# Rotary embedding on one core: 2 MiB units in place of 1 MiB, fp32 stores through ScalarE and SyncE

## The chip, the cores and the metric

The kernel runs on one core of a Trainium2 chip. The metric is the device time of one execution in microseconds (us); 1 us is 1000 ns. An execution is given as the median of several.

## The reference

A rotary position embedding on x of shape (8, 8, 1024, 64), fp32: 64 pairs of batch and head, 1024 positions, 64 values at each. 16.8 MB come in and 16.8 MB go out.

```python
half = x.shape[-1] // 2                       # 32
angles = np.outer(positions * scale, freqs)   # (1024, 32); scale is 0.5
cos, sin = np.cos(angles), np.sin(angles)
x_first, x_second = x[..., :half], x[..., half:]
out_first  = x_first * cos - x_second * sin
out_second = x_first * sin + x_second * cos
out = np.concatenate([out_first, out_second], axis=-1)
```

Positions reach the kernel as 64-bit integers.

## The kernel before

**Units.** A unit is four heads of one batch, 1 MiB of fp32, one contiguous piece of memory. Over 128 partitions each partition has one row of 8 KB: 32 positions of 64 values (`HEADS = 4`, `HP = 32`, `K = 32`, `N = 2048`). There are 16 units (`NU`). Partition p holds positions 32 (p mod 32) and on, so one table of sines and cosines, [128, 32, 32], serves every unit.

**Loads.** Unit 0 comes as fp32 on SP's (SyncE's) queue (L63). The other 15 come in seven DMAs of 1, 1, 2, 2, 3, 3 and 3 units on GpSimd's (POOL's) queue (L78), which cast to fp16 on the way. They are all issued at the start, so all loads stand ahead of every store in that queue. ACT's (ScalarE's) queue brings the positions, the same 8 KB four times, once for each group of 32 partitions (L68), and the row of frequencies (L73).

**Tables.** TensorE spreads the frequencies, times scale / 2 pi, over the partitions (L87, `cfreq`). VectorE (DVE) turns the positions into fp32 (`posf`, L90), multiplies (`y`, L95), and takes off the nearest whole number of turns by adding and subtracting a large constant, once for the sine and once, a quarter turn on, for the cosine (L115, L107, L109). ScalarE takes the sine of both into fp16 tables (L117, L119).

**The loop over units (L124).** Four VectorE instructions a unit: two products of the whole unit with the cosine and with the sine (`pc` L128, `ps` L129, 2048 elements a partition), a difference and a sum of their halves into `OUT`, fp16 (L132, L135, 1024 elements each). `xout` holds ten such buffers. GpSimd's queue stores `OUT` and casts to fp32 on the way (L138). ScalarE has nothing to do in the loop. The tile framework orders the instructions of an engine and places the waits; a buffer is written again only when its last reader has finished, a store when it has landed.

Of the kernel before, what the change touches and what calls it, by code (L numbers as in the profile page):

```python
# [1 line left out]

# [1 line left out]

# [4 lines left out]

FP32 = mybir.dt.float32
FP16 = mybir.dt.float16
I32 = mybir.dt.int32
AF = mybir.ActivationFunctionType
ALU = mybir.AluOpType

_MAGIC = 12582912.0
_TWO_PI_DN = float(np.float32(np.uint32(0x40C90FDA).view(np.float32)))


GROUPS = (1, 1, 2, 2, 3, 3, 3)
BUF_O = 10
BUF_P = 3


@with_exitstack
def kernel(
    ctx: ExitStack,
    tc: tile.TileContext,
    x: bass.AP,  # L30
    freqs: bass.AP,
    positions: bass.AP,
    scale: bass.AP,
    out: bass.AP,
):
    nc = tc.nc

    B, Hh, S, D = x.shape
    NBH = B * Hh
    half = D // 2  # L40
    P = nc.NUM_PARTITIONS
    HEADS = 4
    HP = P // HEADS
    K = S // HP
    N = K * D
    NU = NBH // HEADS
    assert S % HP == 0 and D == 2 * half and NBH % HEADS == 0 and sum(GROUPS) == NU - 1

    fscale = float(scale)

    xv = x.rearrange("b h s d -> (b h s d)").rearrange("(u p n) -> p u n", p=P, n=N)
    ov = out.rearrange("b h s d -> (b h s d)").rearrange("(u p n) -> p u n", p=P, n=N)

    consts = ctx.enter_context(tc.tile_pool(name="consts", bufs=1))
    tmp = ctx.enter_context(tc.tile_pool(name="tmp", bufs=1))
    setup_psum = ctx.enter_context(tc.tile_pool(name="setup_psum", bufs=1, space=bass.MemoryType.PSUM))
    xin = ctx.enter_context(tc.tile_pool(name="xin", bufs=1))
    xout = ctx.enter_context(tc.tile_pool(name="xout", bufs=BUF_O))
    prods = ctx.enter_context(tc.tile_pool(name="prods", bufs=BUF_P))


    X0 = xin.tile([P, N], FP32, name="X0")
    nc.sync.dma_start(out=X0, in_=xv[:, 0, :])  # L63
    xtiles = {0: X0}

    pos_i64 = consts.tile([P, K], positions.dtype)
    for h in range(HEADS):
        nc.scalar.dma_start(  # L68
            out=pos_i64[h * HP : (h + 1) * HP, :],
            in_=positions.rearrange("(q k) -> q k", k=K),  # L70
        )
    freq_row = consts.tile([1, half], FP32)
    nc.scalar.dma_start(out=freq_row, in_=freqs[None, :])  # L73

    u0 = 1
    for g, n in enumerate(GROUPS):
        X = xin.tile([P, n, N], FP16, name=f"X{g + 1}")
        nc.gpsimd.dma_start(out=X, in_=xv[:, u0 : u0 + n, :])  # L78
        for i in range(n):
            xtiles[u0 + i] = X[:, i, :]  # L80
        u0 += n


    coef = consts.tile([1, P], FP32)
    nc.vector.memset(coef, fscale / (2.0 * np.pi))  # L85
    cfreq = setup_psum.tile([P, half], FP32)
    nc.tensor.matmul(out=cfreq, lhsT=coef, rhs=freq_row, start=True, stop=True)  # L87

    posf = consts.tile([P, K], FP32)
    nc.vector.tensor_copy(  # L90
        out=posf,
        in_=pos_i64.bitcast(I32).rearrange("p (k t) -> p k t", t=2)[:, :, 0],
    )
    y = tmp.tile([P, K, half], FP32)
    nc.vector.tensor_tensor(  # L95
        out=y,
        in0=posf.unsqueeze(2).broadcast_to((P, K, half)),
        in1=cfreq.unsqueeze(1).broadcast_to((P, K, half)),
        op=ALU.mult,
    )  # L100

    cosT = consts.tile([P, K, half], FP16)
    sinT = consts.tile([P, K, half], FP16)

    def reduced(src, tag):
        m = tmp.tile([P, K, half], FP32, name="m" + tag)
        nc.vector.tensor_scalar(out=m, in0=src, scalar1=_MAGIC, scalar2=None, op0=ALU.add)  # L107
        rneg = tmp.tile([P, K, half], FP32, name="rneg" + tag)
        nc.vector.scalar_tensor_tensor(  # L109
            out=rneg, in0=m, scalar=_MAGIC, in1=src, op0=ALU.subtract, op1=ALU.subtract  # L110
        )
        return rneg

    yc = tmp.tile([P, K, half], FP32)
    nc.vector.tensor_scalar(out=yc, in0=y, scalar1=0.25, scalar2=None, op0=ALU.add)  # L115
    rc = reduced(yc, "c")
    nc.scalar.activation(out=cosT, in_=rc, func=AF.Sin, bias=0.0, scale=-_TWO_PI_DN)  # L117
    rs = reduced(y, "s")
    nc.scalar.activation(out=sinT, in_=rs, func=AF.Sin, bias=0.0, scale=-_TWO_PI_DN)  # L119
    cos_b = cosT.unsqueeze(2).broadcast_to((P, K, 2, half))  # L120
    sin_b = sinT.unsqueeze(2).broadcast_to((P, K, 2, half))


    for u in range(NU):  # L124
        X = xtiles.pop(u).rearrange("p (k h j) -> p k h j", h=2, j=half)
        pc = prods.tile([P, K, 2, half], FP16, tag="pc")
        ps = prods.tile([P, K, 2, half], FP16, tag="ps")
        nc.vector.tensor_tensor(out=pc, in0=X, in1=cos_b, op=ALU.mult)  # L128
        nc.vector.tensor_tensor(out=ps, in0=X, in1=sin_b, op=ALU.mult)  # L129

        OUT = xout.tile([P, K, 2, half], FP16, tag="O")
        nc.vector.tensor_tensor(  # L132
            out=OUT[:, :, 0, :], in0=pc[:, :, 0, :], in1=ps[:, :, 1, :], op=ALU.subtract
        )
        nc.vector.tensor_tensor(  # L135
            out=OUT[:, :, 1, :], in0=ps[:, :, 0, :], in1=pc[:, :, 1, :], op=ALU.add
        )
        nc.gpsimd.dma_start(out=ov[:, u, :], in_=OUT.rearrange("p k h j -> p (k h j)"))  # L138


# [1 line left out]
_INS = ['x', 'freqs', 'positions', 'scale']  # L142
_OUTS = [((8, 8, 1024, 64), 'float32')]

_NUMBERS = {'scale': 0.5}


# [26 lines left out]
```

## Time and profile before

| what | value |
|---|---|
| median of 11 runs | 85.95 us (85.86 to 86.17) |
| the profiled execution's own time | 85.96 us |
| its span in the profile | 84.2 us |
| VectorE busy | 63.6 us, 76% of the span, 72 instructions |
| ScalarE busy | 3.4 us, 4% |
| GpSimd busy (DMA issue among it) | 13.7 us, 16% |
| HBM read and written | 16.81 MB and 16.78 MB, 399 GB/s over the span |
| GpSimd's DMA queue (q0), share of 16 DMA engines | 99.1% |

The span runs from the first to the last instruction of the profiled execution; its own time has some time outside the span as well. In the profile "DMA" is the busy share of the 16 DMA engines and "GB/s" what they moved, counted at the destination. SPq, ACTq and POOLq are the sequencers that issue DMAs.

### The profile page before, as it was taken

The numbers are of one execution on the slowest core, as the hardware profiler recorded it, in microseconds if no ns is written. First come the engines' busy times: TensorE is split into PE (matmuls) and PEld (weight loads), VectorE is DVE, ScalarE is ACT, GpSimd is POOL, SyncE is SP. The second block draws the span as 40 slices with busy tenths as digits, with TensorE's granted clock in tenths as the row PEclk, the third lists the DMA queues.
The fourth block names the chain that finished last, engine by engine and source line by source line (L and its number), as shares of the span: only waits on it lengthen the run. The fifth ranks groups of instructions, "written<-read, shape, count | busy, mean of one in ns | idle before, by whom it ended". The sixth has DMA issues, their size and how long they took to land.

```text
span 84.2 us, 183 instructions
## 1 busy us (share of the span) xinstructions
PE 0.6 (1%) x2; PEld 0.5 (1%) x2; DVE 63.6 (76%) x72; ACT 3.4 (4%) x3; POOL 13.7 (16%) x27
## 2 busy tenths in 40 slices
PE   0000200000000000000000000000000000000000
PEld 0000100000000000000000000000000000000000
DVE  0000799999999999999999999999999999300000
ACT  0410006300000000000000000000000000000000
POOL 5980000000211202102022020220202202200000
DMA  2899999999999999999999999999999999999970
GB/s 31 311 292 214 208 218 214 212 216 216 214 218 204 218 218 212 214 214 218 177 418 420 436 424 428 424 432 436 420 420 436 420 428 424 436 432 428 420 300 0
DMA packets 4675, 25.73 MB, mean 306 GB/s; under 512 B 578, under 2 KB 578, under 8 KB 2498
## 3 DMA queue, kind: packets, MB, share of 16 engines
q0 software_dynamic: 4336, 24.64, 99.1%
q1 hardware_dynamic: 144, 1.05, 3.6%
q10 hardware_dynamic: 194, 0.03, 0.3%
q14 instruction: 1, 0.01, 0.0%
HBM read 16.81 MB, written 16.78 MB: 399 GB/s over the span
## 4 chain that ended last, share of the span: by engine, by line
DMA 45%; issue 31%; POOL 10%; POOLq 1%
DMA X<-in_x_dram 45%; POOL out_dram L138 5%; POOL X L78 5%; POOLq L169 1%; POOLq L138 0%; POOLq L155 0%
## 5 line engine op out<-in xcount | busy, mean ns | idle before, releaser
L129 DVE TENSOR_TENSOR ps<-X,sinT 128x2048 f16<-128x2048 f16 (+1 forms) x16 | 20.6, 1289 | 0.0
L128 DVE TENSOR_TENSOR pc<-X,cosT 128x2048 f16<-128x2048 f16 (+1 forms) x16 | 20.5, 1287 | 0.0
L138 POOL DMA_DIRECT2D out_dram<-OUT x16 | 8.6, 538 | 58.5 <-DVE OUT L135 58.5
L132 DVE TENSOR_TENSOR OUT<-pc,ps 128x1024 f16<-128x1024 f16 x16 | 11.0, 688 | 0.0
L135 DVE TENSOR_TENSOR OUT<-ps,pc 128x1024 f16<-128x1024 f16 x16 | 11.0, 687 | 0.0
L90 DVE CAST posf<-pos_i 128x32 f32<-128x32 int32 x1 | 0.2, 182 | 7.1 <-DMA pos_i<-in_positions_dram 7.1
L78 POOL DMA_DIRECT2D X<-in_x_dram x7 | 4.9, 714 | 0.8 <-POOLq L155 0.8
L95 DVE TENSOR_TENSOR y<-posf,cfreq 128x1024 f32<-128x1024 f32 x1 | 1.2, 1221 | 0.7 <-PE cfreq L87 0.7
L119 ACT ACTIVATE sinT<-rnegs 128x1024 f16<-128x1024 f32 x1 | 1.1, 1056 | 8.8 <-DVE rnegs L109 8.8
L119 ACT ACT_TABLE_LOAD x1 | 1.3, 1283 | 3.2 <-issue 3.2
L109 DVE SCALAR_TENSOR_TENSOR rnegs<-ms,y 128x1024 f32<-128x1024 f32 x1 | 1.2, 1219 | 0.0
L109 DVE SCALAR_TENSOR_TENSOR rnegc<-mc,yc 128x1024 f32<-128x1024 f32 x1 | 1.2, 1217 | 0.0
L117 ACT ACTIVATE cosT<-rnegc 128x1024 f16<-128x1024 f32 x1 | 1.1, 1057 | 0.1
L85 DVE MEMSET coef<- 1x128 f32 x1 | 0.2, 165 | 0.8 <-PEq L155 0.8
L115 DVE TENSOR_SCALAR yc<-y 128x1024 f32<-128x1024 f32 x1 | 0.7, 693 | 0.0
L107 DVE TENSOR_SCALAR mc<-yc 128x1024 f32<-128x1024 f32 x1 | 0.7, 685 | 0.0
L107 DVE TENSOR_SCALAR ms<-y 128x1024 f32<-128x1024 f32 x1 | 0.7, 684 | 0.0
L87 PE MATMUL cfreq<-freq_row,coef 1*128 1x32 f32 x2 | 0.6, 392 | 8.3 <-DVE posf L90 8.3
L87 PEld LDWEIGHTS cfreq<-freq_row,coef 1*128 1x128 f32 x2 | 0.5, 306 | 8.3 <-DVE posf L90 8.3
L155 POOL MEMSET const-float32-0.0<- 128x1 f32 x1 | 0.1, 98 | 0.2 <-issue 0.2
L155 POOL MEMSET const-bfloat16-1.0<- 128x1 bf16 x1 | 0.1, 101 | 0.0
L155 POOL MEMSET const-float32-1.0<- 128x1 f32 x1 | 0.1, 98 | 0.0
(1 smaller groups left out, 0.1 us busy)
## 6 DMA issues: line engine op xcount, KB each, us to landing
out_dram<-OUT POOLq DMA_DIRECT2D x16, 1024.0 KB, 16.6
X<-in_x_dram POOLq DMA_DIRECT2D x3, 1536.0 KB, 30.6
X<-in_x_dram POOLq DMA_DIRECT2D x2, 1024.0 KB, 15.3
X<-in_x_dram SPq DMA_DIRECT2D x1, 1024.0 KB, 5.0
X<-in_x_dram POOLq DMA_DIRECT2D x2, 512.0 KB, 7.9
pos_i<-in_positions_dram ACTq DMA_DIRECT2D x4, 8.0 KB, 5.0
freq_row<-in_freqs_dram ACTq DMA_DIRECT2D x1, 0.1 KB
```

What stands on the lines that cost most here:

```text
L78: nc.gpsimd.dma_start(out=X, in_=xv[:, u0 : u0 + n, :])
L87: nc.tensor.matmul(out=cfreq, lhsT=coef, rhs=freq_row, start=True, stop=True)
L95: nc.vector.tensor_tensor(out=y, in0=posf.unsqueeze(2).broadcast_to((P, K, half)), in1=cfreq.unsqueeze(1).broadcast_to((P, K, half)), op=A ...
L107: nc.vector.tensor_scalar(out=m, in0=src, scalar1=_MAGIC, scalar2=None, op0=ALU.add)
L109: nc.vector.scalar_tensor_tensor(out=rneg, in0=m, scalar=_MAGIC, in1=src, op0=ALU.subtract, op1=ALU.subtract)
L117: nc.scalar.activation(out=cosT, in_=rc, func=AF.Sin, bias=0.0, scale=-_TWO_PI_DN)
L119: nc.scalar.activation(out=sinT, in_=rs, func=AF.Sin, bias=0.0, scale=-_TWO_PI_DN)
L128: nc.vector.tensor_tensor(out=pc, in0=X, in1=cos_b, op=ALU.mult)
L129: nc.vector.tensor_tensor(out=ps, in0=X, in1=sin_b, op=ALU.mult)
L132: nc.vector.tensor_tensor(out=OUT[:, :, 0, :], in0=pc[:, :, 0, :], in1=ps[:, :, 1, :], op=ALU.subtract)
L135: nc.vector.tensor_tensor(out=OUT[:, :, 1, :], in0=ps[:, :, 0, :], in1=pc[:, :, 1, :], op=ALU.add)
L138: nc.gpsimd.dma_start(out=ov[:, u, :], in_=OUT.rearrange("p k h j -> p (k h j)"))
```

## The change

The kernel is written anew around the same arithmetic:

- A unit is eight heads, 2 MiB; a row is 16 KB, 64 positions a partition. There are eight units, and the table is [128, 64, 32].
- Unit 0 still comes as fp32, half of it on SP's queue, half on ACT's queue behind positions and frequencies. The positions come once, to 16 partitions; TensorE spreads them over the 128 with a mask (`sel`) that GpSimd makes between its first and its second load. ScalarE casts unit 0 to fp16.
- The other seven units are cast loads on GpSimd's queue, one DMA each.
- The cosine comes from the same remainder as the sine: absolute value (a bit operation), then a sine with a bias of a quarter turn.
- Units are worked in the order 1, 2, 0, 3, 4, 5, 6, 7. The four VectorE instructions a unit remain, on twice the elements; all but the sine product write over X.
- ScalarE copies the result into an fp32 buffer `OUT`, of which there are four. Stores move fp32: the first four from GpSimd's queue, the last four from SP's.
- `pin` (`tc.keep_in_program_order`) holds the marked instructions of an engine in the order of the program.

```diff
--- before.py
+++ after.py
@@ -17,10 +17,8 @@
 _MAGIC = 12582912.0
 _TWO_PI_DN = float(np.float32(np.uint32(0x40C90FDA).view(np.float32)))
 
-
-GROUPS = (1, 1, 2, 2, 3, 3, 3)
-BUF_O = 10
-BUF_P = 3
+BUF_O = 4
+BUF_P = 2
 
 
 @with_exitstack
@@ -39,103 +37,113 @@
     NBH = B * Hh
     half = D // 2
     P = nc.NUM_PARTITIONS
-    HEADS = 4
+    HEADS = 8
     HP = P // HEADS
     K = S // HP
     N = K * D
     NU = NBH // HEADS
-    assert S % HP == 0 and D == 2 * half and NBH % HEADS == 0 and sum(GROUPS) == NU - 1
+    assert S % HP == 0 and D == 2 * half and NBH % HEADS == 0
 
     fscale = float(scale)
 
-    xv = x.rearrange("b h s d -> (b h s d)").rearrange("(u p n) -> p u n", p=P, n=N)
-    ov = out.rearrange("b h s d -> (b h s d)").rearrange("(u p n) -> p u n", p=P, n=N)
+    xv = x.rearrange("b h s d -> (b h s d)").rearrange("(u p n) -> u p n", p=P, n=N)
+    ov = out.rearrange("b h s d -> (b h s d)").rearrange("(u p n) -> u p n", p=P, n=N)
 
     consts = ctx.enter_context(tc.tile_pool(name="consts", bufs=1))
     tmp = ctx.enter_context(tc.tile_pool(name="tmp", bufs=1))
-    setup_psum = ctx.enter_context(tc.tile_pool(name="setup_psum", bufs=1, space=bass.MemoryType.PSUM))
+    psum = ctx.enter_context(tc.tile_pool(name="psum", bufs=1, space=bass.MemoryType.PSUM))
     xin = ctx.enter_context(tc.tile_pool(name="xin", bufs=1))
     xout = ctx.enter_context(tc.tile_pool(name="xout", bufs=BUF_O))
     prods = ctx.enter_context(tc.tile_pool(name="prods", bufs=BUF_P))
 
 
-    X0 = xin.tile([P, N], FP32, name="X0")
-    nc.sync.dma_start(out=X0, in_=xv[:, 0, :])
-    xtiles = {0: X0}
 
-    pos_i64 = consts.tile([P, K], positions.dtype)
-    for h in range(HEADS):
-        nc.scalar.dma_start(
-            out=pos_i64[h * HP : (h + 1) * HP, :],
-            in_=positions.rearrange("(q k) -> q k", k=K),
-        )
+    X0f = xin.tile([P, N], FP32, name="X0f")
+    pin = tc.keep_in_program_order
+    nc.sync.dma_start(out=X0f[:, : N // 2], in_=xv[0][:, : N // 2])
+
+    pos_i64 = consts.tile([HP, K], positions.dtype)
+    pin(nc.scalar.dma_start(out=pos_i64, in_=positions.rearrange("(q k) -> q k", k=K)))
     freq_row = consts.tile([1, half], FP32)
-    nc.scalar.dma_start(out=freq_row, in_=freqs[None, :])
+    pin(nc.scalar.dma_start(out=freq_row, in_=freqs[None, :]))
+    pin(nc.scalar.dma_start(out=X0f[:, N // 2 :], in_=xv[0][:, N // 2 :]))
 
-    u0 = 1
-    for g, n in enumerate(GROUPS):
-        X = xin.tile([P, n, N], FP16, name=f"X{g + 1}")
-        nc.gpsimd.dma_start(out=X, in_=xv[:, u0 : u0 + n, :])
-        for i in range(n):
-            xtiles[u0 + i] = X[:, i, :]
-        u0 += n
+    X = [xin.tile([P, K, 2, half], FP16, name=f"X{u}") for u in range(NU)]
+
+    def load(u):
+        nc.gpsimd.dma_start(out=X[u].rearrange("p k h j -> p (k h j)"), in_=xv[u])
+
+
+    sel = consts.tile([HP, HEADS, HP], FP32)
+    load(1)
+    nc.gpsimd.memset(sel, 0.0)
+    nc.gpsimd.affine_select(
+        out=sel, in_=sel, compare_op=ALU.not_equal, fill=1.0, base=0,
+        pattern=[[0, HEADS], [-1, HP]], channel_multiplier=1,
+    )
+    for u in range(2, NU):
+        load(u)
 
 
     coef = consts.tile([1, P], FP32)
-    nc.vector.memset(coef, fscale / (2.0 * np.pi))
-    cfreq = setup_psum.tile([P, half], FP32)
+    pin(nc.vector.memset(coef, fscale / (2.0 * np.pi)))
+    quarter = consts.tile([P, 1], FP32)
+    pin(nc.vector.memset(quarter, np.pi / 2.0))
+    cfreq = psum.tile([P, half], FP32)
     nc.tensor.matmul(out=cfreq, lhsT=coef, rhs=freq_row, start=True, stop=True)
 
+    pos_row = consts.tile([HP, K], FP32)
+    pin(nc.vector.tensor_copy(
+        out=pos_row,
+        in_=pos_i64.bitcast(I32).rearrange("p (k t) -> p k t", t=2)[:, :, 0],
+    ))
+    pos_ps = psum.tile([P, K], FP32)
+    nc.tensor.matmul(
+        out=pos_ps, lhsT=sel.rearrange("q a b -> q (a b)"), rhs=pos_row, start=True, stop=True
+    )
     posf = consts.tile([P, K], FP32)
-    nc.vector.tensor_copy(
-        out=posf,
-        in_=pos_i64.bitcast(I32).rearrange("p (k t) -> p k t", t=2)[:, :, 0],
-    )
+    pin(nc.vector.tensor_copy(out=posf, in_=pos_ps))
+
     y = tmp.tile([P, K, half], FP32)
-    nc.vector.tensor_tensor(
+    pin(nc.vector.tensor_tensor(
         out=y,
         in0=posf.unsqueeze(2).broadcast_to((P, K, half)),
         in1=cfreq.unsqueeze(1).broadcast_to((P, K, half)),
         op=ALU.mult,
-    )
+    ))
+    m = tmp.tile([P, K, half], FP32)
+    pin(nc.vector.tensor_scalar(out=m, in0=y, scalar1=_MAGIC, scalar2=None, op0=ALU.add))
+    r = tmp.tile([P, K, half], FP32)
+    pin(nc.vector.scalar_tensor_tensor(
+        out=r, in0=m, scalar=_MAGIC, in1=y, op0=ALU.subtract, op1=ALU.subtract
+    ))
+    sinT = consts.tile([P, K, half], FP16)
+    pin(nc.scalar.activation(out=sinT, in_=r, func=AF.Sin, bias=0.0, scale=-_TWO_PI_DN))
+    ra = tmp.tile([P, K, half], FP32)
+    pin(nc.vector.tensor_scalar(
+        out=ra.bitcast(I32), in0=r.bitcast(I32), scalar1=0x7FFFFFFF, scalar2=None, op0=ALU.bitwise_and
+    ))
+    cosT = consts.tile([P, K, half], FP16)
+    pin(nc.scalar.activation(out=cosT, in_=ra, func=AF.Sin, bias=quarter, scale=-_TWO_PI_DN))
+    pin(nc.scalar.copy(out=X[0].rearrange("p k h j -> p (k h j)"), in_=X0f))
 
-    cosT = consts.tile([P, K, half], FP16)
-    sinT = consts.tile([P, K, half], FP16)
-
-    def reduced(src, tag):
-        m = tmp.tile([P, K, half], FP32, name="m" + tag)
-        nc.vector.tensor_scalar(out=m, in0=src, scalar1=_MAGIC, scalar2=None, op0=ALU.add)
-        rneg = tmp.tile([P, K, half], FP32, name="rneg" + tag)
-        nc.vector.scalar_tensor_tensor(
-            out=rneg, in0=m, scalar=_MAGIC, in1=src, op0=ALU.subtract, op1=ALU.subtract
-        )
-        return rneg
-
-    yc = tmp.tile([P, K, half], FP32)
-    nc.vector.tensor_scalar(out=yc, in0=y, scalar1=0.25, scalar2=None, op0=ALU.add)
-    rc = reduced(yc, "c")
-    nc.scalar.activation(out=cosT, in_=rc, func=AF.Sin, bias=0.0, scale=-_TWO_PI_DN)
-    rs = reduced(y, "s")
-    nc.scalar.activation(out=sinT, in_=rs, func=AF.Sin, bias=0.0, scale=-_TWO_PI_DN)
     cos_b = cosT.unsqueeze(2).broadcast_to((P, K, 2, half))
     sin_b = sinT.unsqueeze(2).broadcast_to((P, K, 2, half))
 
 
-    for u in range(NU):
-        X = xtiles.pop(u).rearrange("p (k h j) -> p k h j", h=2, j=half)
-        pc = prods.tile([P, K, 2, half], FP16, tag="pc")
+    for i, u in enumerate((1, 2, 0, *range(3, NU))):
         ps = prods.tile([P, K, 2, half], FP16, tag="ps")
-        nc.vector.tensor_tensor(out=pc, in0=X, in1=cos_b, op=ALU.mult)
-        nc.vector.tensor_tensor(out=ps, in0=X, in1=sin_b, op=ALU.mult)
-
-        OUT = xout.tile([P, K, 2, half], FP16, tag="O")
-        nc.vector.tensor_tensor(
-            out=OUT[:, :, 0, :], in0=pc[:, :, 0, :], in1=ps[:, :, 1, :], op=ALU.subtract
-        )
-        nc.vector.tensor_tensor(
-            out=OUT[:, :, 1, :], in0=ps[:, :, 0, :], in1=pc[:, :, 1, :], op=ALU.add
-        )
-        nc.gpsimd.dma_start(out=ov[:, u, :], in_=OUT.rearrange("p k h j -> p (k h j)"))
+        pin(nc.vector.tensor_tensor(out=ps, in0=X[u], in1=sin_b, op=ALU.mult))
+        pin(nc.vector.tensor_tensor(out=X[u], in0=X[u], in1=cos_b, op=ALU.mult))
+        pin(nc.vector.tensor_tensor(
+            out=X[u][:, :, 0, :], in0=X[u][:, :, 0, :], in1=ps[:, :, 1, :], op=ALU.subtract
+        ))
+        pin(nc.vector.tensor_tensor(
+            out=X[u][:, :, 1, :], in0=ps[:, :, 0, :], in1=X[u][:, :, 1, :], op=ALU.add
+        ))
+        OUT = xout.tile([P, N], FP32, tag="O")
+        pin(nc.scalar.copy(out=OUT, in_=X[u].rearrange("p k h j -> p (k h j)")))
+        (nc.gpsimd if i < NU // 2 else nc.sync).dma_start(out=ov[u], in_=OUT)
 
 
 # ---- launch: one core; inputs and outputs as the reference has them ----
```

## The prediction

> **What bounds the kernel now.** First the page: the two DMA rows of the 40 slices (2.1 us each), the queue table, the chain by engine.
>
> ```profile
> span 84.2 us, 183 instructions
> ...
> DVE  0000799999999999999999999999999999300000
> ...
> DMA  2899999999999999999999999999999999999970
> GB/s 31 311 292 214 208 218 214 212 216 216 214 218 204 218 218 212 214 214 218 177 418 420 436 424 428 424 432 436 420 420 436 420 428 424 436 432 428 420 300 0
> ...
> q0 software_dynamic: 4336, 24.64, 99.1%
> ...
> DMA 45%; issue 31%; POOL 10%; POOLq 1%
> ```
>
> The DMA engines are full from slice 2 to slice 37. VectorE (DVE) looks as busy, but stops ten microseconds before the end: it is second. GB/s counts destination bytes: a load that casts to fp16 shows 214 and reads 428, a store shows 428. So both halves run at one rate, 428 GB/s of fp32. The "issue" share of the chain is GpSimd waiting between stores and hides nothing: the transfers behind it had a backlog. The stretches say where DMA time is lost:
>
> ```profile
> core 0: us, PE busy (x) PEld busy (x) DVE busy (x) ACT busy (x) POOL busy (x), PEclk, DMA share, GB/s
> ...
> 1.00:1.50 0.50, 0.00 (x0) 0.00 (x0) 0.00 (x0) 0.00 (x0) 0.26 (x1) 1.00 0.00 0
> ...
> 0.00:5.00 5.00, 0.00 (x0) 0.00 (x0) 0.17 (x1) 1.28 (x1) 3.96 (x10) 1.00 0.61 211
> ...
> 44.00:80.00 36.00, 0.00 (x0) 0.00 (x0) 28.31 (x34) 0.00 (x0) 4.79 (x9) 1.00 1.12 428
> 81.00:81.50 0.50, 0.00 (x0) 0.00 (x0) 0.00 (x0) 0.00 (x0) 0.00 (x0) 1.00 0.80 295
> 81.50:82.00 0.50, 0.00 (x0) 0.00 (x0) 0.00 (x0) 0.00 (x0) 0.00 (x0) 1.00 0.21 66
> 82.00:84.20 2.20, 0.00 (x0) 0.00 (x0) 0.00 (x0) 0.00 (x0) 0.00 (x0) 1.00 0.00 0
> ```
>
> Data flows from about 1.6 to 82.0 us, 80.4 us. Input and output are 33.55 MB; at 428 GB/s that is 78.4 us. The 2.0 us over are a slow start (1.05 MB by 5.0 us instead of 1.46 MB, 0.9 us), an uneven end (0.18 MB in the last microsecond instead of 0.43, 0.6 us), and 0.5 us for the turn from loads to stores and for tiny packets. SP's wait and the landings of the stores say what ends the run:
>
> ```profile
> SPq L169 <- DMA out_dram<-OUT: 81.3, 1, 81.3
> ```
>
> ```profile
> DMA to landing us min/median/max: 9.8/16.6/24.0
> ```
>
> The last store is issued at 72.64 and lands 9.8 us later, at 82.4; the first is issued at 21.5 and lands 24.0 us later, at 45.5, since it stands behind all loads in GpSimd's queue. The span ends 1.7 us after the last landing, and 1.78 us lie outside it (85.96 for a span of 84.18). That run stands at the median (85.95), so I add to 85.96.
>
> **What the Trainium skill says.** "DMA: Bandwidth & Descriptors", section Where 436 GB/s comes from: the ceiling is 435 GB/s over 16 ports; the 428 above agree. The same page, section Why small descriptors are slow (HBM only): each packet has some 3 cycles over its 32-byte beats. An 8 KB row is 256 beats, 301 ns at 850 MHz; one engine's share of 428 GB/s gives 306 ns, so 5 ns a row at most are overhead. The same page, section Queues, rings and completion order: each engine goes round robin between the queues with work, a packet at a time. No row of the trace before shows two large backlogs sharing, so this is taken from the page. "VectorE: DVE Perf Modes", section Side-by-side: where the cycles go for N=2048 bf16, gives 1224 ns for a two-source operation on 16-bit data and 2293 at one element a cycle; here fp16 takes 1222 and fp32 2291.
>
> **The change part by part.** *VectorE.* One unit of now:
>
> ```profile
> 57.03 1.22 DVE L128 TENSOR_TENSOR pc<-X,cosT 128x2048 f16<-128x2048 f16 x1
> 58.16 0.69 DVE L132 TENSOR_TENSOR OUT<-pc,ps 128x1024 f16<-128x1024 f16 x1
> 58.76 0.69 DVE L135 TENSOR_TENSOR OUT<-ps,pc 128x1024 f16<-128x1024 f16 x1
> 59.37 1.22 DVE L129 TENSOR_TENSOR ps<-X,sinT 128x2048 f16<-128x2048 f16 x1
> ```
>
> Starts lie 1.135 us apart for 2048 elements and 0.60 for 1024, also behind a product just written, so working in place should add no wait. 4096 elements take 1.135 + 1.067 = 2.20 (two a cycle at the skill's 0.96 GHz). A new unit takes 2 x 2.20 + 2 x 1.135 = 6.68 us, against 6.95 for two old ones. Half as many instructions save 0.27 us a unit; unit 0 no longer in fp32 saves 2 x 1.07 more. None of it is on the path.
>
> *Set-up.* One positions DMA instead of four.
>
> ```profile
> DMA to landing us min/median/max: 3.4/5.0/5.9
> ```
>
> That row is for the four: each waits for its turn on ACT's queue. I give the only one the shortest, 3.4: it is issued at 0.74 and lands at 4.1 (5.7 with the median). Frequencies follow 0.45 us later, at 4.6, and half of unit 0 behind them. Two matmuls at 0.60 (the present one's time) and a small copy put the angles y at 6.2; y and r have 2048 fp32 elements, 2.29 each (2.20 to the next start), m 1.22 (1.13), so sine starts at 11.9. An ACTIVATE of 1024 elements takes 1.056 now; at the 0.833 ns an element of "ScalarE: Activation LUTs", section What ACT_TABLE_LOAD costs, 2048 take 1.91. The first product starts at 13.9, now 14.4. Units 0 and 1 are 4.2 MB: 1.05 by 5.0 us, the rest at 428, so both have come by 12.8. The mask on GpSimd is not in this trace: between 0.1 us (its memsets) and 2 us, hidden, as the second matmul needs it at 5.3 only. VectorE's units end at 13.9 + 6.68(i+1): 20.6 the first, 47.3 the fifth, 67.3 the last.
>
> *ScalarE.* A copy to fp32 of 4096 elements: 1.056 + 3072 x 0.833 ns = 3.62 us, under VectorE's 6.68, hidden except behind a full set of buffers. The copy of unit 0 ends near 19.5, its product starts at 27.3.
>
> *Stores.* Call them s0 to s7; s0 to s3 stay behind the loads in GpSimd's queue, s4 to s7 go by SP. 2 MiB at 428 GB/s take 4.90. ScalarE has four output buffers, so the copy for s4 waits until s0 has landed, that for s7 until s3 has. Turnaround: landing 0.5, copy 3.62, then SP's issue and start, 0.85 (0.74 to 1.6 for unit 0 now), with waking 5.1 in all. Stores begin near 42.4. s0 ends at 47.3, s1 at 52.2, where s4 begins to share (52.4). Sharing halves s2 and s3: s2 ends at 61.8, s3 at 71.6. By then SP's queue has moved 9.6 us' worth of its 9.8 for s4 and s5, and s6 (copied from 62.4, issued at 66) is behind: 5.1 us of work. s7 can start at 71.6 + 5.1 = 76.7, just when this is used up. So VectorE's 67.3 doesn't matter; the cover of s7's copy is s6, and it has no slack. Bounds on the gap: 0 to 2 us; I take 0.1. What is queued behind the waiting copies on ScalarE is only later copies.
>
> *Rows.* 16 KB instead of 8 KB: an engine's 256 packets become 128, each saving 3.5 ns by the skill's 3 cycles (0.45 us), 5 ns if all excess is by the row (0.64), nothing if rows are cut up or the excess is not by the row. I take 0.3. That a store no longer casts: the byte count on the HBM side is equal and unit 0's uncast load ran at 402 GB/s beside small packets, so 0 (bounds: -0.5 to +1.7, the latter 410 GB/s in 39.2 us of stores). Fewer tiny packets at the start: 0.1 gained. The end is hardware-issued now: 0, from -0.3 to +0.4.
>
> Sum: 85.96 - 0.3 - 0.1 + 0.1 = 85.66, said as **85.65**.
>
> **The rivals.** *A buffer ring that stalls the end (slower).* s7's copy waits for the slowest engine's part of s3. If s3's landing, copy and SP's start take 1.6 us more than the 5.1 us that s6 covers, the DMA idles so long: 87.2. It decides at any excess over 5.1. For it: no slack in my sum; against: were GpSimd's queue served first, s3 would land near 62 and nothing would wait. *Uncast stores that run slower*: twice the SBUF bytes a store; at 410 GB/s 87.6. Against: the skill's ceiling is the same for either. *Rows that don't matter* (the change does not do what it says: rows are cut again, or the 5 ns are not by the row): 85.9. *A better DMA stream*: 0.64 from rows, 0.4 at turn and end: 84.8. *VectorE as the bound*: its end at 67.3 would have to slip beyond 72; lost two-a-cycle speed in place would do it (2 x 2.1 + 2 x 1.07 more a unit), but the shapes are those of now.
>
> **How the numbers follow.** 0.2% (0.17 us) is about what a measurement of this kernel can tell from no change. Likeliest case 0.47 (own range 85.2 to 86.0: faster 0.40, same 0.07); rows that don't matter 0.14 (same 0.09, faster 0.02, slower 0.03); stalled end 0.22 and slow stores 0.10, both slower; better stream 0.07, faster. Together faster 0.49, same 0.16, slower 0.35. The range of all: 84.7 to 87.7.
>
> **What would show it.** Right: DMA tenths of 9 without a dip between 42 and 80, VectorE's last product before 70, ScalarE's copy for s7 waiting on a store's landing near 72, rates of 428 to 432. A dip near 76 shows the stall; rates near 410 slow stores. I am wrong if the first product starts later than 18 or its operations take over 2.4 us.

## The result, and the profile after

The changed kernel takes 84.70 us (median of 8, 84.54 to 84.82) against 85.95 (median of 31): ratio 0.9851, 95% interval 0.9842 to 0.9859. The forecast was 85.65. The direction was right, but the gain is 1.25 us, four times the 0.3 forecast.

The page after, the lines that answer to those shown of before, and the second queue that now stores:

```profile
span 83.3 us, 154 instructions
...
DVE  0008996999999999999999999999999996000000
...
DMA  3899999999999999999999999999999999999990
GB/s 59 283 330 275 295 283 224 220 212 220 216 212 216 212 216 212 224 216 208 142 370 433 417 448 417 448 425 433 433 417 448 417 448 425 433 433 417 448 393 8
...
q0 software_dynamic: 1584, 15.73, 66.6%
q1 hardware_dynamic: 720, 9.44, 27.4%
...
DVE 72%; ACT 7%; DMA 5%; DVEq 1%; PE 1%; issue 1%; ACTq 1%
```

DMA is full as before. Stores show 417 to 448 a slice, mean 432 (it was 428). VectorE heads the chain, since its last product releases ScalarE's last copy and that the last store; what hides behind this, the backlog on SP's queue, the chain doesn't show. The experiments measure it.

This profiled execution took 85.09 us, 0.4 above the median: one DMA engine ended 0.4 us after the rest. A second profile of the same kernel (`after_again`, 84.58 us) doesn't have this and is used from here on. Its stretches, in the columns of the table of stretches before:

```profile
0.00:5.00 5.00, 0.00 (x0) 0.00 (x0) 0.40 (x3) 1.28 (x1) 3.87 (x12) 1.00 0.67 215
...
44.00:70.00 26.00, 0.00 (x0) 0.00 (x0) 25.72 (x16) 13.05 (x4) 0.53 (x1) 1.00 1.01 432
44.00:80.00 36.00, 0.00 (x0) 0.00 (x0) 26.00 (x16) 16.65 (x5) 0.53 (x1) 1.00 1.01 431
```

The first five microseconds are hardly better than before (215 for 211), the stores are a little faster (431 for 428 in the same stretch). Its stores on the output tensor:

```profile
L146 SPq DMA_DIRECT2D out_dram<-OUT x4: 332/332/337, 53.2 to 74.0; - x4
...
DMA to landing us min/median/max: 7.9/16.3/22.1
```

The last store is issued at 74.0 and lands 7.9 us later, at 81.9; before it was 82.4. The span of this execution is 82.8 us. So in this profile 0.5 us of the gain lie ahead of the last landing and 0.85 behind it: from landing to the end of the span it was 1.75 us and is 0.9. The 0.85 is the firm part: in the first profile after, the last landing is at 82.4 as before the change, and 0.84 of its 0.87 us of gain lie behind it. The view of the kernel's last line (the end of the program; start times of the first and last of each kind stand behind the durations) shows what happens there. Before:

```profile
L169 SPq EVENT_SEMAPHORE  x10: 17/28/28, 82.4 to 84.1; - x10
L169 POOLq EVENT_SEMAPHORE  x4: 17/17/17, 83.5 to 84.1; - x4
L169 POOLq DRAIN  x3: 45/93/10803, 72.6 to 83.9; - x3
```

After (second profile):

```profile
L177 SPq EVENT_SEMAPHORE  x11: 17/28/28, 74.4 to 82.7; - x11
L177 POOLq EVENT_SEMAPHORE  x4: 17/17/17, 82.1 to 82.7; - x4
L177 POOLq DRAIN  x3: 45/93/21937, 46.5 to 82.5; - x3
```

GpSimd's first DRAIN starts behind its last store and holds it until its own queue is done. Before it starts at 72.61 and takes 10.80 us: it ends at 83.42, 0.98 us after the last landing, and only then does GpSimd join the others at the end (83.5). After, it ends at 46.5 + 21.9 = 68.4, long before the last landing, and GpSimd joins at 82.1.

SP comes second. An EVENT_SEMAPHORE of SP is here a wait, for a DMA's landing or for the other engines. Before, eight waits for landings lie behind the last landing, 0.06 us apart: the first starts at 82.45, the last ends at 82.92, half a microsecond ahead of GpSimd's DRAIN. After, only one does; the others began at 74.4 and were through before. So the 0.85 needed both. Had the DRAIN alone gone, the seven more waits would have left an end of about 1.33 us (an estimate: 0.89 and seven times 0.0625); kernels below with three and five such waits end at 1.01 and 1.14, as this counting gives.

These lines of before stood in the trace when the prediction was made.

Below, "end" is the time from the last landing (the trace's DMA records) to the end of the span. Between the span and the device time lie 1.78 us in both kernels (84.18 to 85.96, 82.80 to 84.58).

### The profile page after: what moved, and what is told of

Read it like the earlier page. It is cut to its first block, busy times and chain, and to the rows that moved or that the text cites. A ratio compares the mean times of both kernels' runs of the same rounds, so it can differ in the third digit from the quotient of the medians.

```text
span 83.3 us, 154 instructions
## 1 busy us (share of the span) xinstructions
PE 1.1 (1%) x4; PEld 0.9 (1%) x4; DVE 62.6 (75%) x40; ACT 37.4 (45%) x12; POOL 6.7 (8%) x17
## 4 chain that ended last, share of the span: by engine, by line
DVE 72%; ACT 7%; DMA 5%; DVEq 1%; PE 1%; issue 1%; ACTq 1%
DVE X L137 22%; DVE ps L136 21%; DVE X L138 12%; DVE X L141 10%; DMA freq_row<-in_freqs_dram 5%; ACT OUT L145 4%; DVE r L117 3%; DVE y L108 3%; ACT sinT L121 2%; DVE m L115 1%; DVEq L177 1%; PE cfreq L93 1%; PE pos_ps L101 1%; ACTq L66 0%; DVE posf L105 0%
## 5 line engine op out<-in xcount | busy, mean ns | idle before, releaser
L145 ACT CAST OUT<-X 128x4096 f32<-128x4096 f16 x8 | 28.8, 3606 | 25.0 <-DVE X L141 25.0
L136 DVE TENSOR_TENSOR ps<-X,sinT 128x4096 f16<-128x4096 f16 x8 | 18.3, 2285 | 0.7 <-ACT sinT L121 0.7
L137 DVE TENSOR_TENSOR X<-X,cosT 128x4096 f16<-128x4096 f16 x8 | 18.3, 2292 | 0.3
L138 DVE TENSOR_TENSOR X<-X,ps 128x2048 f16<-128x2048 f16 x8 | 9.8, 1225 | 0.3
L141 DVE TENSOR_TENSOR X<-ps,X 128x2048 f16<-128x2048 f16 x8 | 9.7, 1218 | 0.0
L146 POOL DMA_DIRECT2D out_dram<-OUT x4 | 2.1, 534 | 39.1 <-ACT OUT L145 39.1
L128 ACT CAST X<-X0f 128x4096 f16<-128x4096 f32 x1 | 3.6, 3590 | 0.0
L117 DVE SCALAR_TENSOR_TENSOR r<-m,y 128x2048 f32<-128x2048 f32 x1 | 2.3, 2293 | 0.0
L108 DVE TENSOR_TENSOR y<-posf,cfreq 128x2048 f32<-128x2048 f32 x1 | 2.3, 2289 | 0.0
L127 ACT ACTIVATE cosT<-ra,quarter 128x2048 f16<-128x2048 f32 x1 | 2.0, 1987 | 0.0
```

The source lines that it names most:

```text
L108: pin(nc.vector.tensor_tensor(out=y, in0=posf.unsqueeze(2).broadcast_to((P, K, half)), in1=cfreq.unsqueeze(1).broadcast_to((P, K, half)), ...
L117: pin(nc.vector.scalar_tensor_tensor(out=r, in0=m, scalar=_MAGIC, in1=y, op0=ALU.subtract, op1=ALU.subtract))
L128: pin(nc.scalar.copy(out=X[0].rearrange("p k h j -> p (k h j)"), in_=X0f))
L136: pin(nc.vector.tensor_tensor(out=ps, in0=X[u], in1=sin_b, op=ALU.mult))
L137: pin(nc.vector.tensor_tensor(out=X[u], in0=X[u], in1=cos_b, op=ALU.mult))
L138: pin(nc.vector.tensor_tensor(out=X[u][:, :, 0, :], in0=X[u][:, :, 0, :], in1=ps[:, :, 1, :], op=ALU.subtract))
```

## The experiments

All are made from the changed kernel, but for `b_half_sp`. The times are medians beside the kernel before on the same chip (85.89 to 86.01).

**`all_pool`: all stores from GpSimd.**

```diff
-        (nc.gpsimd if i < NU // 2 else nc.sync).dma_start(out=ov[u], in_=OUT)
+        nc.gpsimd.dma_start(out=ov[u], in_=OUT)
```

> All eight fp32 stores go by GpSimd's queue instead of four. Theory (the end): in the profile before, GpSimd's last wait ends about 1.0 us after the last store has landed, in the profile after 0.2 us, since its own queue had finished long before; so most of the gain lies behind the last landing. Then this kernel loses about 0.85 us: 85.5 us, with about 1.7 us from the last landing to the end of the span. Rival (the stream): hardware-issued stores or uncast stores move data faster; then the time from the last landing to the end is not what changes, stores here run at 428 instead of 432 GB/s in the last 20 us, and the loss is at most 0.2 us: 84.9.

Measured: 85.09 us. The last landing is at 81.9, as in the second profile after. The end is 1.39 us:

```profile
L177 POOLq DRAIN  x3: 45/88/8389, 74.2 to 83.0; - x3
```

The DRAIN ends at 82.56, 0.65 us after the landing. So the engine that issues does nothing for the stream, and about 0.45 us for the end (0.5 by the profiles): half of what was expected, for 0.65 is less than the 0.98 of before. `pool_split` below asks why.

**`cast_pool`: no copies on ScalarE, casting stores from GpSimd.**

```diff
-        OUT = xout.tile([P, N], FP32, tag="O")
-        pin(nc.scalar.copy(out=OUT, in_=X[u].rearrange("p k h j -> p (k h j)")))
-        (nc.gpsimd if i < NU // 2 else nc.sync).dma_start(out=ov[u], in_=OUT)
+        nc.gpsimd.dma_start(out=ov[u], in_=X[u].rearrange("p k h j -> p (k h j)"))
```

> As after the change, but stores are fp16 from X, cast to fp32 by GpSimd's DMA as in the kernel before; ScalarE copies nothing in the loop and all eight stores go by GpSimd. If stores that don't cast neither gain nor lose, this equals the kernel with all fp32 stores by GpSimd: 85.1. If casting slows the stream (the 428 GB/s of before against 434), 85.4 to 85.6. If the end depends on the cast, the time from the last landing to the end differs from 1.39 us.

Measured: 85.12 us, last landing 81.9, end 1.39: equal to `all_pool` in all three. A store that casts is neither slower nor faster. So ScalarE's copies earn nothing by themselves; in the changed kernel they serve the stores on SP's queue.

**`rows8`: rows of 8 KB again.**

```diff
-        nc.gpsimd.dma_start(out=X[u].rearrange("p k h j -> p (k h j)"), in_=xv[u])
+        xf = X[u].rearrange("p k h j -> p (k h j)")
+        for c in (slice(0, N // 2), slice(N // 2, N)):
+            nc.gpsimd.dma_start(out=xf[:, c], in_=xv[u][:, c])
...
-        (nc.gpsimd if i < NU // 2 else nc.sync).dma_start(out=ov[u], in_=OUT)
+        for c in (slice(0, N // 2), slice(N // 2, N)):
+            (nc.gpsimd if i < NU // 2 else nc.sync).dma_start(out=ov[u][:, c], in_=OUT[:, c])
```

> Every load on GpSimd's queue and every store is cut into two DMAs of half the columns, so that rows are 8 KB again; all else is as after the change. Theory: rows give the part of the gain that the end does not, 3.5 to 5 ns for each of 128 more packets an engine, 0.45 to 0.6 us: 85.2. Rival: the row length does nothing and the stream is faster for the engine that issues or for lack of a cast: 84.7.

Measured: 85.38 us, 0.75 above `after_again` (84.63, on another chip). The stretch of stores:

```profile
44.00:70.00 26.00, 0.00 (x0) 0.00 (x0) 25.72 (x16) 13.05 (x4) 1.05 (x2) 1.00 1.01 428
```

428 GB/s, as before the change, and the last landing is at 82.3. Only a part of the 0.75 us is the rows. 0.25 us is the end, 1.14 here: after the last landing SP still has four more waits, 0.06 us each, for DMAs that have long landed. Another 0.27 us lies outside the span, 2.05 us in this kernel and 1.77 to 1.78 in every other profile; why is open. That leaves 0.23 us for the stream by the medians. By the landings it is 0.4 against the second profile after, and 0.3 against the mean (82.0) of the six profiles that have 16 KB rows and the set-up of the change, with stores from GpSimd or from both (`after`, `after_again`, `all_pool`, `cast_pool`, `sp_last2`, `sp_last3`: 81.9 to 82.4). So rows are worth 0.2 to 0.4 us.

**`all_sp`: all stores from SP.** The line of `all_pool` with `nc.sync`.

> All eight fp32 stores go by SP's queue, so the first three share the DMA engines with the loads instead of standing behind them. Theory (the end): the time from the last landing to the end stays at 0.9 us, and the stream is as full: 84.7, within 0.3. Rival (hardware-issued stores stream better): a further 0.2 to 0.4 us faster, 84.4. A third possibility is that reads and writes mixed from 26 us on are slower than a single turn near 41 us: 85.5 or more.

Measured: 85.13 us (85.03 to 85.73). None of the expected numbers: last landing 82.2, end 1.14, again with four more waits on SP behind the landing. Reads and writes mixed from 29 us on, where the first store's rows go, show no large cost, and more hardware-issued stores no gain. The landing is 0.3 us later than in `after_again`, within what two profiles of the changed kernel differ (81.9 and 82.4).

**`b_half_sp`: the end alone, in the kernel before.**

```diff
-        nc.gpsimd.dma_start(out=ov[:, u, :], in_=OUT.rearrange("p k h j -> p (k h j)"))
+        if u < NU // 2:
+            nc.gpsimd.dma_start(out=ov[:, u, :], in_=OUT.rearrange("p k h j -> p (k h j)"))
+        else:
+            OUTF = xoutf.tile([P, N], FP32, tag="OF")   # a pool of 5
+            nc.scalar.copy(out=OUTF, in_=OUT.rearrange("p k h j -> p (k h j)"))
+            nc.sync.dma_start(out=ov[:, u, :], in_=OUTF)
```

> The kernel before, with one thing taken over from the change: its last eight 1 MiB stores are copied to fp32 by ScalarE and go by SP's queue; rows stay 8 KB, the set-up and VectorE's work as they were. Theory (the end): GpSimd's queue is done before the last landing, so that the 1.75 us from the last landing to the end shrink to 0.9 to 1.2, by how many waits SP still has after the last landing; the stream is that of before: 85.2 (85.1 to 85.4). Rival (the stream gains by row length and set-up, the end by nothing): 85.95.

Measured: 85.36 us against 85.89, ratio 0.9938 (0.9919 to 0.9958). The last landing is at 82.5, as before; the end is 1.0, with two more waits of SP. This line alone, put into the old kernel, takes off 0.5 us by the median and 0.7 by the profile (span 83.5 for 84.2). Its DRAIN starts behind GpSimd's last store at 46.1:

```profile
L175 POOLq DRAIN  x3: 39/99/22207, 46.1 to 83.2; - x3
```

It ends at 68.3, 0.66 us after the last landing of GpSimd's own queue (67.66), and so the end of before is not a constant.

**`pool_split`: what the DRAIN goes by.**

```diff
-            nc.gpsimd.dma_start(out=ov[u], in_=OUT)       # the line of all_pool
+        for c in (slice(0, P // 2), slice(P // 2, P)):
+            nc.gpsimd.dma_start(out=ov[u][c, :], in_=OUT[c, :])
```

> All stores on GpSimd's queue as fp32, each cut into two DMAs of 64 partitions, so 16 stores and 7 loads by GpSimd as in the kernel before, with rows of 16 KB. Idea: GpSimd's last instruction ends 0.98 us after the last landing with 23 DMAs on its queue (before) and 0.65 us with 15 (all stores by GpSimd), 43 ns a DMA both times. If it goes by DMAs, 0.98 us here, 1.7 us from landing to end, 85.4. If it goes by rows or bytes (here 1920 rows, as with whole stores), 0.65 us and 85.1.

Measured: 94.1 us, which nothing had foretold: stores of 64 partitions move at 332 GB/s between 44 and 70 us, with the DMA engines as busy (share 1.00) as with 434 in `all_pool`:

```profile
44.00:70.00 26.00, 0.00 (x0) 0.00 (x0) 25.72 (x16) 13.08 (x4) 4.27 (x8) 1.00 1.00 332
...
L178 POOLq DRAIN  x3: 45/88/16491, 74.7 to 91.7; - x3
```

For its own question the run is good: the last landing is at 90.21, the DRAIN ends at 91.19, 0.98 us later, and the end is 1.72. Four kernels agree on 43 ns a DMA on GpSimd's queue: 23 DMAs give 0.98 (before and here), 15 give 0.65 (`all_pool`, `cast_pool`), with 3968 and 1920 rows for the same 0.98. All four have seven loads on that queue, and the two with 23 have stores of 1 MiB, so these four alone can't tell loads from stores, or the size of a DMA from the number of DMAs. The other traces, where the DRAIN comes before the end, can. From the last landing on GpSimd's queue to the DRAIN's end it is 0.33 us for 7 DMAs, loads alone (`all_sp`), 0.49 for 11 (`after_again`), 0.57 for 13 (`sp_last2`), 0.66 for 15, with stores of 1 MiB (`b_half_sp`), and 0.94 for 22, 14 of them loads (`rows8`): 43 to 47 ns each in all of them. So it goes by DMAs, loads and stores alike, not by rows or bytes. What GpSimd does for each is not visible.

**`xfirst`: half of unit 0 ahead of positions and frequencies.**

```diff
+    pin(nc.scalar.dma_start(out=X0f[:, N // 2 :], in_=xv[0][:, N // 2 :]))
     pos_i64 = consts.tile([HP, K], positions.dtype)
     ...
-    pin(nc.scalar.dma_start(out=X0f[:, N // 2 :], in_=xv[0][:, N // 2 :]))
```

> The second half of unit 0 is issued ahead of positions and frequencies on ACT's queue. Theory: positions land near 7 to 8 us instead of 3.9, the first product starts 4 us later (18.5), the last copy on ScalarE starts near 74 instead of 70.2; the last store then starts about 1.3 us after the backlog on SP's queue has run out: 86.0. Rival (VectorE and set-up have more slack than that, and two queues of large rows from 0.75 us on fill the slow start better): 84.4.

Measured: 90.53 us. Positions land 11.0 us after issue, not 6 to 7, as they stand behind 1 MiB that shares its turn with two other queues. The timeline:

```profile
12.22 0.18 DVE L96 CAST pos_row<-pos_i 16x64 f32<-16x64 int32 x1 [11.22 <-DMA pos_i<-in_positions_dram]
...
21.90 2.29 DVE L136 TENSOR_TENSOR ps<-X,sinT 128x4096 f16<-128x4096 f16 x1 [0.72 <-ACT sinT L121]
...
77.52 3.60 ACT L145 CAST OUT<-X 128x4096 f32<-128x4096 f16 x1 [3.32 <-DVE X L141]
```

Against the second profile after, the first product (14.74 there) and the last copy (70.36) are 7.2 us late, and the end of this profiled execution (90.06 us) 5.5. Some 1.7 us were slack. The start gains nothing: 48 and 271 GB/s in the first two slices.

**`dve_split`: eight VectorE instructions a unit.**

```diff
+        for c in (slice(0, K // 2), slice(K // 2, K)):
+            Xc, pc = X[u][:, c], ps[:, c]
-        pin(nc.vector.tensor_tensor(out=ps, in0=X[u], in1=sin_b, op=ALU.mult))
+            pin(nc.vector.tensor_tensor(out=pc, in0=Xc, in1=sin_b[:, c], op=ALU.mult))
...
```

> As after the change, but VectorE works each unit in two halves, eight instructions a unit of half the size: the number of instructions of before. About 0.07 us for each of 32 more instructions, 2.2 us, put the last product near 72.2 instead of 70.1. Theory (VectorE is off the path with some 2 us to spare, as the kernel with unit 0 issued first shows: 7.3 us later at the first product cost 5.8): 84.7 to 85.1. Rival (VectorE's shorter work is where the gain comes from, it heads the chain of the profile after): 86.5 or more.

Measured: 87.57 us: my number was too low. Halves cost 0.52 us a unit (7.44 from unit to unit for 6.92), not 0.28, so the last copy starts at 74.95 instead of 70.36:

```profile
74.95 3.60 ACT L147 CAST OUT<-X 128x4096 f32<-128x4096 f16 x1 [3.84 <-DVE X L143]
```

4.6 us later at the copy, 2.9 at the end: 1.7 us of slack, as in `xfirst`. The backlog says the same: SP's wait for s6 in `after_again` ends near 77.1, so s6's data ends near 76.7; s7, issued at 74.0, could start near 75. So the rival had a part of the truth: in this arrangement half as many instructions are needed to keep VectorE off the path, though they bring no gain by themselves.

**`after_again`, `sp_last2`, `sp_last3`: how many stores must go by SP.**

```diff
-        (nc.gpsimd if i < NU // 2 else nc.sync).dma_start(out=ov[u], in_=OUT)
+        (nc.gpsimd if i < NU - 2 else nc.sync).dma_start(out=ov[u], in_=OUT)    # NU - 3
```

> The changed kernel once more, as the measure for the two that follow on the same chip: 84.7 us.

> As after the change, but only the last two stores go by SP's queue and the first six by GpSimd's. If the end is what matters, GpSimd's queue must only be done before the last landing (its sixth store near 75 us): the end stays at 0.9 us, and a shorter time with two queues side by side may leave the DMA engines more even at the end, as with all stores on one queue, where the last landing came at 81.9: 84.5 to 84.7. Rival (half of the stores must be hardware-issued for the gain): 84.9 or more.

> The same with the last three stores on SP's queue: between the two, 84.5 to 84.7; rival 84.8 or more.

Measured: 84.63, 84.66 and 84.71 us, all with an end of 0.9: no difference (0.2% is 0.17 us). Two stores by SP are enough, as GpSimd's DRAIN then ends near 74, well before the last landing. No version was found that beats the changed kernel.

## Why the prediction was wrong

**The bound.** Right: the DMA engines, in both kernels.

**The end: the step that failed.** "The end is hardware-issued now: 0, from -0.3 to +0.4." It measured -0.85. The prediction read the last landing (82.4) and the end of the span, and carried the 1.7 us between them over as a constant (the 1.78 us outside the span are the same in both kernels). It asked who issues the last store, and not what each engine still waits for. The signs that it named came true, but for the wait on a landing near 72 (no dip of the DMA, 432 GB/s, VectorE done with its products before 70), and none of them looked behind the last landing. In place of the 0 the runs show GpSimd's DRAIN and SP's waits behind the last landing. Of the 0.85, `b_half_sp` takes off 0.73 in the old kernel (1.75 to 1.01); the other 0.12 are its two more waits of SP. `all_pool` gives 0.5 of the 0.85 back in the new kernel; it does not give all of it back, since 15 DMAs stand on GpSimd's queue where there were 23.

**Rows.** Right: 0.3 taken, 0.2 to 0.4 by `rows8`, within the bounds 0 to 0.64. By the 3 cycles a packet of the Trainium skill ("DMA: Bandwidth & Descriptors", section Why small descriptors are slow (HBM only)) the estimate was 0.45, somewhat more than measured.

**Start.** 0.1 taken: `rows8`, with old rows and the new start, lands at 82.3, before at 82.4. This fits, but the landings of one kernel differ by more, so it is not shown.

**Uncast stores.** 0 as taken: `cast_pool` equals `all_pool`. The rival at 87.6 is out. (By the prediction's own terms, 85.66 and 1.7, it stood at 87.4.)

**The gap at s7.** 0.1 taken, none there, for another reason than mine. I let s4 take its turns 0.85 us after its issue. In the DMA records of the second profile it is issued at 53.2, its first row goes at 56.9, and only then do rows of s2, s3 and SP's queue alternate one by one. This agrees with the round robin by packets that the Trainium skill states ("DMA: Bandwidth & Descriptors", section Queues, rings and completion order), with a row as the packet. Why the first row waits 3.7 us is not shown; the engines may have had some rows of the full queue on hand. GpSimd's last row ends at 67.0, s3 lands at 67.9 and not at 72.1, and the copy for s7 waited for VectorE alone: all 25.0 us of ScalarE's waits in the loop are put down to it, none to a landing. The stalled end of 87.2 does not occur. The point from which VectorE decides (72) was about right: 70.3 for its last result and 1.7 us of slack.

**VectorE.** A unit was to take 6.68 us and takes 6.92. In the timeline of the first profile after, the columns as before:

```profile
49.25 2.28 DVE L136 TENSOR_TENSOR ps<-X,sinT 128x4096 f16<-128x4096 f16 x1
51.56 2.29 DVE L137 TENSOR_TENSOR X<-X,cosT 128x4096 f16<-128x4096 f16 x1
...
53.89 1.22 DVE L138 TENSOR_TENSOR X<-X,ps 128x2048 f16<-128x2048 f16 x1
55.03 1.22 DVE L141 TENSOR_TENSOR X<-ps,X 128x2048 f16<-128x2048 f16 x1
```

The product over X starts 2.31 us after the one before, and the difference 2.33 after it, each when its predecessor has ended (2.28 and 2.29), not 0.09 before that as elsewhere. "Working in place should add no wait" was wrong by 0.24 us a unit, 1.9 us in all; the slack hid it. That it is the writing in place that does this was not tried alone, and it is not the only case: in the set-up of the second profile `m`, which reads the `y` just written and writes elsewhere, also starts only at 9.21, when `y` has ended (9.18). The first product, said for 13.9, starts at 14.7, as the frequencies land at 5.4 and not at 4.6.

The sum as it should have been, by the profiles: 85.96 - 0.5 (rows and start, the last landing at 81.9 for 82.4) - 0.85 (end) = 84.6; the second profile says 84.58.

**Near by luck.** The rival of a better DMA stream, 84.8, came nearest, but not for its reason: it had 0.64 for rows, where 0.2 to 0.4 was measured, and 0.4 at turn and end, where 0.85 came from behind the last landing, which is no part of the stream.

## What to carry to other kernels

Read the time behind the last landing as its own stage: which engine joins the end last, what its last DRAIN waits for, and which engine would be last without it. Let GpSimd's queue run dry before the last landing, by giving the last two stores to SP's queue, and keep the DMAs few: each on GpSimd's queue cost 43 ns where that DRAIN was last, each wait that SP still had after the last landing cost 0.06 us where no DRAIN came later. When DMA bounds both versions, less work on VectorE is slack and no gain; its worth is found by making it slower until the end moves.

## What the runs showed of the hardware that I had not expected

- GpSimd's DRAIN ends some 43 to 47 ns for each DMA of its queue after the last landing on that queue: 0.33 us for 7, 0.49 for 11, 0.65 for 15, 0.94 for 22, 0.98 for 23.
- Each wait that SP still had behind the last landing took 0.06 us, also for a DMA that had long landed: with one the end was 0.89 us, with three 1.01, with five 1.14.
- Stores of 64 partitions, two for each unit on one queue, move at 332 GB/s where one of 128 partitions moves at 432 to 434.
- A DMA issued on a second queue beside a full one sent its first row 3.7 us after its issue in `after_again` and 6.1 in `b_half_sp` (51.3 to 57.4); at the start of the kernel, on idle engines, it took 1.0.
- A positions DMA of 8 KB landed 3.1 us after its issue at the head of ACT's queue and 11.0 behind 1 MiB.
